# Two heads' chunk matrices side by side on one diagonal, inverted and folded together, in a one-core RWKV-7 + sparse-attention layer

## The chip, the cores and the metric

The kernel runs on one core of one Trainium2 chip. The metric is the device time of one execution in microseconds (us). The core has five engines that run side by side and wait for one another through semaphores: PE (TensorE, the matrix multiplier; its weight loads are listed apart as PEld), DVE (VectorE), ACT (ScalarE), POOL (GpSimd) and SP (SyncE, which here issues the transfers).

## What is computed

One layer of a decoder: 512 prompt tokens and 64 sample tokens (8 requests of 8), width 1024, with two token mixers on the same normalised input, a gated merge, an output projection and a SwiGLU network. The change lies in the first mixer, RWKV-7, whose state S (64x64 for each of 8 heads) goes from token to token:

```
def step(S, inp):
    r_t, w_t, k_t, v_t, a_t, b_t = inp
    sa = einsum('bhij,bhj->bhi', S, a_t)
    S = S * w_t[:, :, None, :] + sa[..., None] * b_t[:, :, None, :] + v_t[..., None] * k_t[:, :, None, :]
    return S, einsum('bhij,bhj->bhi', S, r_t)
```

The kernel takes 64 tokens at a time (a chunk). Within a chunk the term `sa` of a token depends on those of the tokens before it, which makes a triangular 64x64 system, identity minus N; its inverse is multiplied ("folded") into the read vectors, and then only 8 short steps for the prompt, and one for the samples, are left of the recurrence.

## The kernel before, in words

The 8 heads are worked on in 4 pairs i = 0..3, each with 9 chunks (8 of the prompt, the ninth of the samples), so 18 units of chunk and head. For each pair:

- `rw_operands` makes the scaled vectors, and by matmuls (L581, L592) the products of each chunk with itself. `pairs_out` masks them out of PSUM on DVE, in three instructions for four chunks of one head. The matrix N goes to partitions 64 to 127 of the tile `gb`, one 64x64 block for each of the 18 units.
- `rw_inverse` sends the four 16x16 diagonal blocks of each N through DRAM (`d1`) into 36 rows of the tile `im`, inverts them all with 30 DVE instructions (tiles `im`, `iw`, `invt`), and brings them back through DRAM (`d2`) into `gb`, `dt` (the tile `invt`), `b1` (named `b` in the rows) and `wt` (named `yb`). Its transfers are issued by SP in the order of its queue: 4 to `d1`, 1 from it, 2 to `d2`, 7 from it.
- `rw_merge_inverse` builds the 32x32 and then the 64x64 inverse from the blocks, on PE, in partitions 64 to 127, nine units (`u0` = 0, then 9) at a time: L661, evacuation L664, L668 and L671, evacuations L673 and L676, then L680, L683, L686, L688.
- `rw_transposed_reads` transposes the read vectors (L696) into `at`, a tile for each head, and `rw_fold_inverse` multiplies them by the inverse (L704), one product per unit, evacuates (L706), and clears the lower half of `gb` on POOL (L708).
- `rw_chain` runs the 8 steps (L803, L807, L812, L821), then the samples.

PE works on whatever the order gives it. Between the steps of the recurrence stand dense products of the input projection (L359, tile `pd`, here called fill): `spares` and `pull` hand out 26 tiles of it, by the tables `FILL` (how many tiles before chain i) and `PULL` (how many pieces after each half step). A list scheduler then orders all instructions on each engine; the functions `fold(i)` and parts of the chain have high priority in it. The fill counts 1968 dense matmuls up to its end, which lies within chain 3. After it come the attention heads (L1186 to L1227), the merge, the output projection and the feed-forward network, all with dense products on PE. Every 32-bit matmul of the small steps shows in the trace as two records, a transpose as one.

Of the kernel before, what the change touches and what calls it, by code (L numbers as in the profile page):

```python
# [13 lines left out]
F32R = mybir.dt.float32r  # L14
# [88 lines left out]
FILL = (12, 0, 6, 2)  # L103
PULL = (3, 5, 3, 2)
# [4 lines left out]
def tile_hybrid_step(ctx: ExitStack, tc: tile.TileContext, I: dict, O: dict):  # L109
# [372 lines left out]
    state, inv, bks = [], [], []  # L482

    def rw_tiles():

        state.extend(block(x, "state") for x in "XY")
        inv.extend(wide(x, x) for x in ("im", "iw"))
        bks.extend(wide(x, x) for x in ("bk0", "bk1"))

    def rw_state_tiles(i):  # L490
# [9 lines left out]
        S["agh"] = t_[:, 0:2 * w].rearrange("p (h c x) -> p c h x", h=2, c=9)  # L500
        S["lam"] = slots.t(32, "lam", "lam", 2).rearrange("p (h c) -> p h c", h=2)
        return S

    def pairs_out(pv_, mk, gb, ag):

        n = pv_.shape[1]
        for (rows, x) in ((slice(64, 128), 0), (slice(0, 64), 64)):
            tt(V, gb[rows], pv_[0:64, :, x:x + 64], bc(mk[0:64, None, x:x + 64], [64, n, 64]), ALU.mult)
        tt(V, ag[64:128], pv_[64:128], bc(mk[64:128, None, :], [64, n, 128]), ALU.mult)

    def rw_operands(S, i):
# [53 lines left out]
        for h in range(2):  # L565
# [27 lines left out]
        pairs_out(pt[:, 0:256].rearrange("p (h x) -> p h x", x=128), gmask[1], S["gb"][:, 8], S["agh"][:, 8])  # L593
# [11 lines left out]
    def rw_inverse(S):  # L605
# [32 lines left out]
        for k in range(2):
            o = 64 + k * 32
            G.tensor_copy(S["b1"][o:o + 16, :, 0:16], bc(ident[o:o + 16, None, o:o + 16], [16, NU, 16]))  # L640
            dma(S["dt"][o:o + 16], d2[1, k, :, 0].rearrange("u s t -> s u t"))
        for k in range(2):
            o = 64 + k * 32
            dma(S["b1"][o + 16:o + 32, :, 16:32], d2[0, k, :, 1].rearrange("u s t -> s u t"))
        dma(S["wt"][80:96, :, 16:32], d2[1, 0, :, 1].rearrange("u s t -> s u t"))
        for k in range(2):
            o = k * 32 + 16
            dma(gu[64 + o:80 + o, :, o:o + 16], d2[0, k, :, 1].rearrange("u s t -> s u t"))

    def rw_merge_inverse(S):  # L650

        gu, dt, b1, wt = S["gb"].rearrange("p c h x -> p (c h) x"), S["dt"], S["b1"], S["wt"]
        for k in range(2):
            o = k * 32
            G.tensor_copy(gu[64 + o:80 + o, :, o:o + 16], bc(ident[64 + o:80 + o, None, 64 + o:80 + o], [16, NU, 16]))
        for u0 in (0, 9):
            pz = PS(S["ct"])
            for u in range(9):
                for k in range(2):
                    o = k * 32  # L660
                    MM(pz[64 + o:96 + o, u * 16:u * 16 + 16], lhsT=gu[64 + o:80 + o, u0 + u, o:o + 32],  # L661
                       rhs=dt[64 + o:80 + o, u0 + u], start=True, stop=True)
            zt = slots.t(512, f"zt{S['i']}", f"zt{S['par']}")
            A.copy(zt[64:128, 0:144], pz[64:128, 0:144])  # L664
            pw = PS(S["ct"])
            for u in range(9):
                z0 = zt[64:96, u * 16:u * 16 + 16]
                MM(pw[64:96, 288 + u * 16:304 + u * 16], lhsT=b1[64:96, u0 + u], rhs=z0, start=True, stop=True)  # L668
                for k in range(2):
                    o = 64 + k * 32  # L670
                    MM(pw[o:o + 16, u * 32:u * 32 + 32], lhsT=zt[o:o + 32, u * 16:u * 16 + 16], rhs=b1[o:o + 32, u0 + u],  # L671
                       start=True, stop=True)
            V.tensor_copy(wt[64:96, u0:u0 + 9, 0:16], pw[64:96, 288:432].rearrange("p (u t) -> p u t", t=16))  # L673
            for k in range(2):
                o = k * 32
                A.copy(gu[64 + o:80 + o, u0:u0 + 9, o:o + 32], pw[64 + o:80 + o, 0:288].rearrange("p (u t) -> p u t", t=32))  # L676
        for u0 in (0, 9):
            pz = PS(S["ct"])
            for u in range(9):
# [1081 lines left out]
```

## Time and profile before

| | us |
|---|---|
| three runs | 1177.23, 1191.52 (median), 1199.91 |
| profiled execution | 1183.65 |
| its span, first to last instruction | 1181.8 |
| PE busy in it | 1128.9 (96%) |
| DVE busy | 729.4 (62%) |

A busy PE is not PE at its peak: matmuls overlap, and a stage of small ones is busy throughout. Start-to-start times in the timeline say more than durations. The column PEclk is the granted TensorE clock: 1.00 is 2.4 GHz, 0.50 is 1.2 GHz.

### The profile page before, as it was taken

Reading aid. Unit: us, or ns where it says so; the run is one execution under the profiler, and the core shown is the slowest. Engines: PE = TensorE matmul, PEld = TensorE weight load, DVE = VectorE, ACT = ScalarE, POOL = GpSimd, SP = SyncE. Lnnn points to the kernel's source line nnn. Section 1 sums busy time; section 2 is a strip of 40 time slices with the busy share of each in tenths; the row PEclk is TensorE's granted clock in tenths of the full one; section 3 lists DMA queues with packets and bytes.
Section 4 is the critical chain, followed back from the end, with each engine's and each line's share of the span. In section 5 each row is a group of like instructions: output and inputs, shape, how many; then the busy total and the mean of one; then the engine's idle time right before and its main releaser. Section 6 shows DMA issues by size and latency. Waiting matters only on the chain.

```text
span 1181.8 us, 23148 instructions
## 1 busy us (share of the span) xinstructions
PE 1128.9 (96%) x9117; PEld 1067.7 (90%) x9117; DVE 729.4 (62%) x1461; ACT 523.9 (44%) x1096; POOL 244.5 (21%) x313
## 2 busy tenths in 40 slices
PE   6999899999999999889999999999999999999995
PEld 5889899999888989777787999999999999999995
DVE  5484835359593754785677665697546754377554
ACT  4554533364533433675676433574223331234232
POOL 3333120024332221642254122100000100001000
PEclk9999999999987999899999999999999999999998
DMA  7223333222252353512331553314323242132222
GB/s 183 75 59 97 77 88 94 57 59 69 77 145 83 87 133 90 138 31 83 112 104 53 165 152 89 109 37 133 102 70 90 72 142 73 56 89 72 90 72 81
DMA packets 194792, 108.95 MB, mean 92 GB/s; under 512 B 49780, under 2 KB 187970, under 8 KB 194682
## 3 DMA queue, kind: packets, MB, share of 16 engines
q1 hardware_dynamic: 194682, 107.46, 32.7%
q8 instruction: 72, 1.18, 0.4%
q14 instruction: 38, 0.31, 0.1%
HBM read 91.40 MB, written 16.02 MB: 91 GB/s over the span
## 4 chain that ended last, share of the span: by engine, by line
PE 80%; DVE 8%; ACT 4%; DMA 4%; issue 2%; SPq 2%; POOL 0%; POOLq 0%; ACTq 0%; DVEq 0%
PE pd L359 46%; PE pu L359 10%; PE acc L1216 2%; PE ps L704 2%; PE ps L581 2%; SPq L152 1%; PE pT L1201 1%; PE ps L1037 1%; PE pS L1186 1%; DMA wraw<-in_w_in 1%; PE sm L396 1%; DVE invt L155 1%; PE pS L1188 1%; PE pq L733 1%; PE ps L696 1%
## 5 line engine op out<-in xcount | busy, mean ns | idle before, releaser
L359 PE MATMUL pd<-hh,whi 128*128 128x256 f32 (+1 forms) x656 | 203.7, 311 | 8.8 <-ACT pe L407 4.3
L359 PE MATMUL pd<-hh,wlo 128*128 128x256 f32 (+1 forms) x656 | 202.8, 309 | 2.7 <-DVE wlo L155 1.6
L359 PE MATMUL pd<-hl,whi 128*128 128x256 f32 (+1 forms) x656 | 201.5, 307 | 0.0
L359 PE MATMUL pd<-act,hi 128*128 128x288 f32 (+2 forms) x704 | 141.8, 296 | 0.0
L359 PEld LDWEIGHTS pd<-hh,whi 128*128 128x128 f32 x656 | 128.5, 196 | 11.9 <-ACT pe L407 6.3
L359 PEld LDWEIGHTS pd<-hh,wlo 128*128 128x128 f32 x656 | 128.5, 196 | 5.1 <-DVE wlo L155 2.0
L359 PEld LDWEIGHTS pd<-hl,whi 128*128 128x128 f32 x656 | 128.7, 196 | 1.4
L359 PEld LDWEIGHTS pd<-act,hi 128*128 128x128 f32 x704 | 112.6, 188 | 0.1
L155 DVE TENSOR_TENSOR wlo<-wraw,whi 128x1024 fp32r<-128x1024 f32 x60 | 81.0, 1351 | 43.8 <-ACT whi L337 40.0
L359 PE MATMUL pd<-act,lo 128*128 128x288 f32 (+2 forms) x352 | 103.8, 296 | 0.0
L359 PE MATMUL pd<-h2l,hi 128*128 128x288 f32 x352 | 103.6, 295 | 0.0
L359 PE MATMUL pd<-h2h,hi 128*128 128x288 f32 x352 | 103.1, 295 | 0.0
L359 PE MATMUL pd<-h2h,lo 128*128 128x288 f32 x352 | 103.1, 294 | 0.0
L337 ACT CAST hi<-wraw 128x1024 fp32r<-128x1024 f32 (+1 forms) x46 | 46.5, 1012 | 118.8 <-PE pd L359 62.5
L337 ACT CAST whi<-wraw 128x1024 fp32r<-128x1024 f32 x59 | 61.8, 1047 | 83.2 <-PE pd L359 52.7
L155 POOL TENSOR_TENSOR sg<-sg,ut 128x576 f32<-128x576 f32 x11 | 18.1, 1646 | 340.6 <-DVE ut L155 325.5
L155 DVE TENSOR_TENSOR x<-x,pd 128x288 f32<-128x288 f32 (+1 forms) x64 | 28.8, 451 | 65.4 <-PE pd L359 65.4
L155 DVE TENSOR_TENSOR lo<-wraw,hi 128x1024 fp32r<-128x1024 f32 (+1 forms) x46 | 57.0, 1240 | 19.0 <-ACT hi L337 18.8
L359 PEld LDWEIGHTS pd<-h2l,hi 128*128 128x128 f32 x352 | 66.1, 188 | 0.0
L359 PEld LDWEIGHTS pd<-act,lo 128*128 128x128 f32 x352 | 66.0, 188 | 0.0
L359 PEld LDWEIGHTS pd<-h2h,lo 128*128 128x128 f32 x352 | 66.0, 188 | 0.0
L359 PEld LDWEIGHTS pd<-h2h,hi 128*128 128x128 f32 x352 | 65.9, 188 | 0.0
(539 smaller groups left out, 2920.1 us busy)
## 6 DMA issues: line engine op xcount, KB each, us to landing
wraw<-in_w_in SPq DMA_DIRECT2D x35, 512.0 KB
wraw<-in_w_ffn_gate SPq DMA_DIRECT2D x22, 512.0 KB
ur<-in_w_ffn_up SPq DMA_DIRECT2D x44, 256.0 KB
wraw<-in_w_ffn_down SPq DMA_DIRECT2D x16, 512.0 KB
gt<-gsp SPq DMA_DIRECT2D x16, 288.0 KB
xt<-in_x_prompt SPq DMA_DIRECT2D x8, 512.0 KB
wraw<-in_w_out SPq DMA_DIRECT2D x8, 512.0 KB
wraw<-in_w_ffn_down SPq DMA_DIRECT2D x8, 384.0 KB
```

Of the source, the lines that this page charges most:

```text
L152: (eng or nc.sync).dma_start(out, in_)
L155: return e.tensor_tensor(out, a, b, op)
L337: e[0](hi[:, 0:n], raw[:, 0:n])
L359: i_ = MM(pt[:, 0:w_], lhsT=w, rhs=x[:, c], start=first and k == 0 and j == 0, stop=last and k == n - 1 and j == 2, **kw)
L396: MM(pt[:, 0:HALF], lhsT=l, rhs=r[:, half(a)], start=i == 0, stop=i == len(terms) - 1)
L581: MM(pt[:, c * 128:(c + 1) * 128], lhsT=bk[0:64, c0 + c], rhs=ag[:, c0 + c], start=True, stop=True)
L696: TR(pt[0:64, c * 128:c * 128 + 128], S["ag"][h][:, c0 + c, 0:64], ident)
L704: MM(pw[:, x * 64:x * 64 + 64], lhsT=S["at"][h][:, c], rhs=S["gb"][64:128, c, h], start=True, stop=True)
L733: MM(pq4[0:64, h, :, b], lhsT=s0s[h][0:64, b * 64:b * 64 + 64], rhs=rv[:, :, b], start=True, stop=True)
L1037: MM(po, lhsT=w[:, sl_], rhs=z[:, l, :, hf:hf + 162], start=hf == 0 and l == 0 and j == 0, stop=hf == 1 and l == 7 and j == 2)
L1186: MM(pS[:, 0:nk], lhsT=qs[:, qt * 128:qt * 128 + 128], rhs=kh[:, 0:nk], start=True, stop=False, skip_group_check=True)
L1216: MM(po[:, c0:hf * 256 + 256], lhsT=lv, rhs=ptx[m][:, kk * 256 + q0:kk * 256 + 256], start=name == "slc" and hf == 0 and kt == 0 and j == ...
```

## The change

The matrices N of both heads of a pair now go into one 128x128 tile per chunk, `nb`: head 0 in rows and columns 0 to 63, head 1 in 64 to 127, zeros elsewhere (set once). So there are 9 units instead of 18, and each of the 32-row quarters of PE holds a piece. The merge runs in one round over four quarters instead of two rounds over two. Both heads' transposed reads stand one above the other in one tile `at` of 128 partitions, and the fold is one product of 128x128 by 128x128 per chunk, for both heads. `gb` keeps zeros in its lower half for good, so the clearing after the fold goes. The transfers become twice as many where a head now has its own partitions (8, 1, 2 and 14 instead of 4, 1, 2 and 7), each of half the size. `pairs_out` is called once per head for the ninth chunk. The tiles `im` and `iw` shrink; the keys of the attention move into `bk0`, `bk1` and the values into `at0`, `at1`. `FILL` and `PULL` get other numbers, and the software DMA scratch is set to 2048.

```diff
-FILL = (12, 0, 6, 2)
-PULL = (3, 5, 3, 2)
+FILL = (10, 2, 6, 2)
+PULL = (4, 4, 3, 2)
...
-        inv.extend(wide(x, x) for x in ("im", "iw"))
+        inv.extend(slots.t(512, x) for x in ("im", "iw"))
...
+        nbs.extend(wide(x, x).rearrange("p (c x) -> p c x", x=128) for x in ("nb0", "nb1"))
+        ats.extend(wide(x, x).rearrange("p (c x) -> p c x", x=128) for x in ("at0", "at1"))
+        for t_ in nbs:
+            G.memset(t_, 0.0)
+        for t_ in state:
+            G.memset(t_[64:128, 4 * NTOK:8 * NTOK], 0.0)
...
-        for (rows, x) in ((slice(64, 128), 0), (slice(0, 64), 64)):
-            tt(V, gb[rows], pv_[0:64, :, x:x + 64], bc(mk[0:64, None, x:x + 64], [64, n, 64]), ALU.mult)
+        q = slice(h * 64, h * 64 + 64)
+        tt(V, nb[q, :, q], pv_[0:64, :, 0:64], bc(mk[0:64, None, 0:64], [64, n, 64]), ALU.mult)
+        tt(V, gb[0:64], pv_[0:64, :, 64:128], bc(mk[0:64, None, 64:128], [64, n, 64]), ALU.mult)
...
-        for k in range(2):
+        units = [(slice(h * 9, h * 9 + 9), k, h * 64 + k * 32) for h in range(2) for k in range(2)]
+        for u, k, o in units:
             for b in range(2):
-                o = k * 32 + b * 16
-                dma(d1[k, :, b].rearrange("u s t -> s u t"), gu[64 + o:80 + o, :, o:o + 16])
+                q = slice(o + b * 16, o + b * 16 + 16)
+                dma(d1[k, u, b].rearrange("u s t -> s u t"), nb[q, :, q])
...
+        for u, k, o in units:
+            G.tensor_copy(S["b1"][o:o + 16, :, 0:16], bc(ident[o:o + 16, None, o:o + 16], [16, 9, 16]))
+            dma(S["dt"][o:o + 16], d2[1, k, u, 0].rearrange("u s t -> s u t"))
+        for u, k, o in units:
+            dma(S["b1"][o + 16:o + 32, :, 16:32], d2[0, k, u, 1].rearrange("u s t -> s u t"))
+            if k == 0:
+                dma(S["wt"][o + 16:o + 32, :, 16:32], d2[1, 0, u, 1].rearrange("u s t -> s u t"))
+        for u, k, o in units:
+            q = slice(o + 16, o + 32)
+            dma(nb[q, :, q], d2[0, k, u, 1].rearrange("u s t -> s u t"))
...
+        quarters, halves = (0, 32, 64, 96), (0, 64)
...
+        for u in range(9):
+            for o in quarters:
+                MM(pz[o:o + 32, u * 16:u * 16 + 16], lhsT=nb[o:o + 16, u, o:o + 32], rhs=dt[o:o + 16, u], start=True, stop=True)
...
+            for o in quarters:
+                MM(pw[o:o + 16, u * 32:u * 32 + 32], lhsT=z[o:o + 32], rhs=b1[o:o + 32, u], start=True, stop=True)
+            for o in halves:
+                MM(pw[o:o + 32, 288 + u * 16:304 + u * 16], lhsT=b1[o:o + 32, u], rhs=z[o:o + 32], start=True, stop=True)
...
+            for o in halves:
+                MM(pz[o + 32:o + 64, u * 32:u * 32 + 32], lhsT=nb[o:o + 32, u, o + 32:o + 64], rhs=wt[o:o + 32, u],
...
+                MM(pw[o:o + 32, u * 32:u * 32 + 32], lhsT=zt[q, u * 32:u * 32 + 32], rhs=nb[q, u, q], start=True, stop=True)
...
-        for cs in ([(c, 0) for c in range(8)], [(c, 1) for c in range(8)], [(8, h) for h in range(2)]):
+        for c0 in (0, 4, 8):
+            m = min(4, 9 - c0)
             pw = PS(S["ct"])
-            for x, (c, h) in enumerate(cs):
-                MM(pw[:, x * 64:x * 64 + 64], lhsT=S["at"][h][:, c], rhs=S["gb"][64:128, c, h], start=True, stop=True)
...
-        G.memset(S["gb"][64:128], 0.0)
+            for c in range(m):
+                MM(pw[:, c * 128:c * 128 + 128], lhsT=S["at"][:, c0 + c], rhs=S["nb"][:, c0 + c], start=True, stop=True)
```

Below, pieces of the order of instructions are shown; the number after a tile's name only tells one buffer from another. First PE at the fold of pair 0, before: `im` and `iw` are the two heads' transposed reads, `state` holds the inverse, and `pd` is fill.

```order
958 L704 MATMUL ps_1585<-state_316,im_318 128x64 x3
959 L704 MATMUL ps_1595<-state_316,iw_319 128x64 x8
960 L600 MATMUL ps_1342<-ident_63,bk_85_320 128x64
961 L600 MATMUL ps_1342<-ident_63,bk_86_321 128x64
962 L696 MATMUL ps_1424<-ident_63,state_317 64x128 x4
963 L359 MATMUL pd_2070<-hh_98,wlo_2039 128x320
964 L359 MATMUL pd_2070<-hh_100,whi_2038 128x320
965 L359 MATMUL pd_2070<-hl_101,whi_2038 128x320
966 L704 MATMUL ps_1605<-state_316,im_318 128x64
```

The same place on PE now (L715 is the fold):

```order
934 L359 MATMUL pd_2095<-hl_97,whi_2063 128x320
935 L359 MATMUL pd_2095<-hh_96,wlo_2064 128x320
936 L715 MATMUL ps_1620<-nb_87_322,at_89_324 128x128 x4
937 L715 MATMUL ps_1626<-nb_87_322,at_89_324 128x128 x4
938 L612 MATMUL ps_1369<-ident_63,bk_85_320 128x64
939 L612 MATMUL ps_1369<-ident_63,bk_86_321 128x64
940 L706 MATMUL ps_1467<-ident_63,state_317 64x128
941 L706 MATMUL ps_1470<-ident_63,state_317 64x128
```

The products of 64 columns become half as many of 128 columns, from one pair of tiles. The next piece is SP's queue where pair 0's inverse comes back from DRAM, before (`state` is `gb`):

```order
136 L152 DMA d2p_158_897<-iw_319 36x512
137 L152 DMA d2p_158_897<-im_318 36x512
138 L152 DMA nsp<-nsp_1879 128x320
139 L152 DMA b_160_940<-d2p_158_897 16x18x16
140 L152 DMA invt_906<-d2p_158_897 16x18x16 x2
141 L152 DMA b_160_940<-d2p_158_897 16x18x16
142 L152 DMA yb_941<-d2p_158_897 16x18x16
143 L152 DMA state_316<-d2p_158_897 16x18x16 x2
```

And now:

```order
136 L152 DMA d2p_162_908<-iw_319 36x512
137 L152 DMA d2p_162_908<-im_318 36x512
138 L152 DMA nsp<-nsp_1994 128x320
139 L152 DMA b_164_955<-d2p_162_908 16x9x16
140 L152 DMA invt_921<-d2p_162_908 16x9x16 x4
141 L152 DMA yb_956<-d2p_162_908 16x9x16
142 L152 DMA b_164_955<-d2p_162_908 16x9x16 x2
143 L152 DMA yb_956<-d2p_162_908 16x9x16
144 L152 DMA b_164_955<-d2p_162_908 16x9x16
145 L152 DMA nb_87_322<-d2p_162_908 16x9x16 x4
```

Seven transfers become fourteen in the same place of the queue. Over the whole program the order has 311 places, instead of 285, at which PE passes between fill and another matmul before the fill ends, and four steps of chain 3, instead of three, begin after the end of the fill.

## Rows read from the trace of the kernel before

**Rows 1.** The page's first two parts: busy time of each engine, then the granted clock of PE in 40 slices of the span, in tenths.

```profile
PE 1128.9 (96%) x9117; PEld 1067.7 (90%) x9117; DVE 729.4 (62%) x1461; ACT 523.9 (44%) x1096; POOL 244.5 (21%) x313
...
PEclk9999999999987999899999999999999999999998
```

**Rows 2.** The chain of work that ended last, by engine, shares of the span.

```profile
PE 80%; DVE 8%; ACT 4%; DMA 4%; issue 2%; SPq 2%; POOL 0%; POOLq 0%; ACTq 0%; DVEq 0%
```

**Rows 3.** Windows of 100 us and more: from:to, length, busy us (instructions) of PE, PEld, DVE, ACT, POOL, then the granted clock, the DMA share and GB/s.

```profile
100.00:200.00 100.00, 95.68 (x938) 90.12 (x937) 55.13 (x133) 42.35 (x84) 22.12 (x38) 0.97 0.35 86
200.00:300.00 100.00, 100.00 (x934) 94.90 (x933) 59.92 (x123) 46.57 (x99) 24.40 (x25) 0.98 0.23 63
300.00:400.00 100.00, 97.50 (x902) 90.00 (x901) 60.66 (x133) 43.32 (x87) 32.32 (x40) 0.90 0.39 104
400.00:500.00 100.00, 94.50 (x879) 86.30 (x877) 61.99 (x153) 43.63 (x114) 30.40 (x38) 0.91 0.45 118
```

**Rows 4.** The timeline of PE at the fold (L704) of pair 0, and at four transposes with a full 128x128 operand (L848): start us, us from the first start to the last end, and the count of records.

```profile
178.56 1.61 PE L704 MATMUL ps<-state,iw 64*128 64x64 f32 x13
...
354.88 0.66 PE L848 MATMUL ps<-ident,yb 128*128 128x128 f32 x4
```

**Rows 5.** Groups by line and shape on PE: busy us, mean ns of one record, idle before.

```profile
L704 PE MATMUL ps<-state,bk 64*128 64x64 f32 x72 | 10.1, 284 | 0.0
...
L686 PE MATMUL ps<-state,zt 32*32 32x32 f32 x144 | 6.2, 192 | 0.0
L704 PE MATMUL ps<-state,iw 64*128 64x64 f32 x36 | 6.2, 330 | 0.0
...
L704 PE MATMUL ps<-state,im 64*128 64x64 f32 x36 | 5.5, 288 | 0.0
```

**Rows 6.** The timeline of PE in the merge: 16-column products that alternate between two 32-row quarters (L661), 32-column products in one quarter (L686).

```profile
159.68 0.71 PE L661 MATMUL ps<-invt,state 16*32 16x16 f32 x35
...
174.10 0.75 PE L686 MATMUL ps<-state,zt 32*32 32x32 f32 x18
```

**Rows 7.** The timeline of PE where it passes from fill to eight small products (64 rows) and back.

```profile
151.92 0.31 PE L359 MATMUL pd<-hh,whi 128*128 128x320 f32 x1
152.07 0.30 PE L359 MATMUL pd<-hl,whi 128*128 128x320 f32 x1
152.30 1.16 PE L581 MATMUL ps<-state,bk 64*128 64x128 f32 x8
153.39 0.42 PE L359 MATMUL pd<-hh,wlo 128*128 128x320 f32 x1
153.64 0.31 PE L359 MATMUL pd<-hh,whi 128*128 128x320 f32 x1
```

**Rows 8.** SP's queue at pair 0: the issue of the four transfers to `d1`, then of the seven back from `d2`.

```profile
113.00 2.06 SPq L152 DMA_DIRECT2D d1p<-state  x4
...
150.62 0.32 SPq L152 DMA_DIRECT2D b<-d2p  x1
151.04 0.90 SPq L152 DMA_DIRECT2D invt<-d2p  x2
151.99 0.44 SPq L152 DMA_DIRECT2D b<-d2p  x1
152.53 0.40 SPq L152 DMA_DIRECT2D yb<-d2p  x1
152.97 0.95 SPq L152 DMA_DIRECT2D state<-d2p  x2
```

**Rows 9.** DVE's three instructions of `pairs_out` for the ninth chunk.

```profile
112.57 1.04 DVE L155 TENSOR_TENSOR state<-ps,mat 64x128 f32<-64x128 f32 x3
```

**Rows 10.** POOL's clearing after the fold (ns: least, median, most; then first and last start).

```profile
L708 POOL MEMSET state<- x4: 1052/1054/1063, 182.3 to 442.8; 64x1152 f32 x4
```

**Rows 11.** Windows of 5 us where PE stood idle or the granted clock fell, and one (175 to 180) where it did not (columns as in rows 3).

```profile
130.00:135.00 5.00, 1.67 (x10) 1.46 (x10) 4.77 (x20) 4.50 (x9) 0.52 (x3) 0.95 0.15 49
...
160.00:165.00 5.00, 5.00 (x55) 4.43 (x49) 2.95 (x5) 2.80 (x6) 0.00 (x0) 0.68 0.51 141
...
175.00:180.00 5.00, 5.00 (x43) 4.74 (x44) 1.50 (x8) 1.87 (x5) 0.42 (x1) 1.00 0.17 43
...
335.00:340.00 5.00, 2.50 (x19) 2.19 (x18) 4.96 (x10) 0.95 (x3) 1.11 (x2) 0.93 0.49 126
...
370.00:375.00 5.00, 5.00 (x49) 4.64 (x46) 1.65 (x4) 1.56 (x3) 0.00 (x0) 0.85 0.62 166
375.00:380.00 5.00, 5.00 (x26) 4.43 (x26) 1.53 (x3) 1.43 (x3) 2.60 (x2) 0.50 0.00 1
380.00:385.00 5.00, 5.00 (x33) 4.71 (x32) 1.06 (x4) 0.72 (x2) 1.34 (x5) 0.63 0.08 26
425.00:430.00 5.00, 5.00 (x50) 4.47 (x50) 4.21 (x9) 1.04 (x3) 0.43 (x2) 0.69 0.76 200
440.00:445.00 5.00, 5.00 (x29) 4.23 (x29) 1.23 (x1) 2.89 (x7) 1.05 (x1) 0.67 0.00 0
445.00:450.00 5.00, 5.00 (x30) 5.00 (x31) 0.28 (x1) 0.66 (x2) 0.00 (x0) 0.64 0.59 162
485.00:490.00 5.00, 2.01 (x13) 1.59 (x13) 3.70 (x13) 2.61 (x10) 4.62 (x9) 0.95 0.38 87
```

**Rows 12.** The steps of chain 3 (L803, tile `qy3c`): duration of one record in ns, first and last start in us.

```profile
L803 PE MATMUL qy3c<-state x32: 217/275/422, 445.6 to 495.8; 128*128 128x64 f32 x32
```

More of the change, by code (lines that the diff above doesn't have):

```diff
@@ L592, in rw_operands @@
             MM(pt[:, h * 128:(h + 1) * 128], lhsT=bk2[h][0:64, 8], rhs=S["ag"][h][0:64, 8], start=True, stop=True)
-        pairs_out(pt[:, 0:256].rearrange("p (h x) -> p h x", x=128), gmask[1], S["gb"][:, 8], S["agh"][:, 8])
+        p3 = pt[:, 0:256].rearrange("p (h x) -> p h x", x=128)
+        for h in range(2):
+            pairs_out(p3[:, h:h + 1], gmask[1], h, S["nb"][:, 8:9], S["gb"][:, 8:9, h], S["ag"][h][:, 8:9])
         for h in range(2):
@@ L608, in rw_inverse @@
         d2 = scratch.tile([2, 2, NU, 2, 16, 16], F32, name=nm(f"d2p{S['i']}"), tag="d2", bufs=2)
-        gu = S["gb"].rearrange("p c h x -> p (c h) x")
+        nb = S["nb"]
         mt, wt = inv
-        S["at"] = [t_[64:128].rearrange("p (c x) -> p c x", x=128) for t_ in (bks if S["par"] else inv)]
         n = 2 * NU
@@ L636, in rw_inverse @@
-        for t_ in (S["b1"][64:128], S["wt"][64:96]):
+        S["wt"] = S["yb"][:, 0:288].rearrange("p (u t) -> p u t", t=32)
+        for t_ in (S["b1"], S["wt"]):
             tc.add_manual_dep(G.memset(t_, 0.0).ins, S["scaled"].ins.name, ORDER, reason="behind the scalings")
[L638 to L648, printed above, removed]
-    def rw_merge_inverse(S):
[L652 to L679, printed above, removed]
-                MM(pz[96:128, u * 32:u * 32 + 32], lhsT=gu[64:96, u0 + u, 32:64], rhs=wt[64:96, u0 + u],
-                   start=True, stop=True)
-            zt = slots.t(512, f"zt{S['i']}", f"zt{S['par']}")
-            A.copy(zt[96:128, 0:288], pz[96:128, 0:288])
-            pw = PS(S["ct"])
-            for u in range(9):
-                MM(pw[64:96, u * 32:u * 32 + 32], lhsT=zt[96:128, u * 32:u * 32 + 32], rhs=gu[96:128, u0 + u, 32:64],
-                   start=True, stop=True)
-            A.copy(gu[64:96, u0:u0 + 9, 32:64], pw[64:96, 0:288].rearrange("p (u t) -> p u t", t=32))
@@ L690, in rw_transposed_reads @@
     def rw_transposed_reads(S):
-        for h in range(2):
-            for c0 in (0, 4, 8):
-                m = min(4, 9 - c0)
+        for c0 in (0, 4, 8):
+            m = min(4, 9 - c0)
+            for h in range(2):
                 pt = PS(S["ct"])
@@ L1097, in ns_operands @@
             vr = projected(2 * bi + 1, C(name="vraw"))
-            vt = wide(f"bk{bi}", "vtok")
+            vt = wide(f"at{bi}", "vtok")
             N.setdefault("vt", []).append(vt)
@@ L1742 @@
     from concourse.bass_utils import run_bass_kernel_spmd
[L1744 removed]
+    nc = bacc.Bacc("TRN2", target_bir_lowering=False, num_devices=1, dynamic_dma_scratch_size=2048)
     arrays, ins, outs = {}, {}, {}
```

49 lines of the change are left out of this document (37 added, 12 removed).

## The prediction

> **What bounds the kernel now.** I read the page first. PE is busy for 96% of the span and no other engine for more than 62% [rows 1], and the chain that ended last is PE for 80% of it [rows 2]. So this is a kernel of PE work, and the question is whether the stage of the change is that too. The windows say that it is: from 100 to 500 us, where all four pairs are worked on, PE is busy 388 of 400 us, with DVE at 55 to 62 and ACT at 42 to 47 in each 100 [rows 3]. The reader is to see there that the recurrence, a chain full of waits, is already covered: between its steps PE does fill. A wait that becomes shorter in this stage is worth little; PE time that goes is worth all of itself, as long as fill is left. What spoils the picture is the granted clock: 0.90 and 0.91 in the second half of the stage [rows 3], with single windows at 0.50, which is 1.2 GHz, although PE was busy in them [rows 11].
>
> **The change part by part.**
>
> *The fold.* It has 72 + 36 + 36 = 144 records [rows 5], 36 products for each pair. Thirteen of them take 1.61 us; less the length of one (0.28 us, by the mean of 284 ns) that is 1.33 / 12 = 0.111 us from start to start [rows 4, 5]. Now there are 9 products for each pair, 72 records, with a full 128x128 operand and 128 columns. The nearest row is a transpose with the same operand and columns: (0.66 - 0.28) / 3 = 0.127 us [rows 4]. So 144 x 0.111 - 72 x 0.127 = 16.0 - 9.1 = 6.8 us less. A product may cost more than a transpose. If a record with twice the columns took twice as long, nothing would be gained; if it took the old 0.111, 8.0 us would be. I take the transpose's value, since its operand and columns are the same.
>
> *The second half of the merge.* L686 works in one quarter of PE, with 32 columns: (0.75 - 0.19) / 17 = 0.033 us from start to start [rows 5, 6]. L680 has as many products, by the code, so 288 records in all. Now they alternate between two quarters. Where two quarters already alternate (L661, 16 columns) it is (0.71 - 0.19) / 34 = 0.015 us [rows 6]. I take 0.020, near that row because of the alternation and above it because of the columns: 288 x 0.013 = 3.7 us less. Ends: 0, if a quarter's neighbour doesn't help, and 288 x 0.018 = 5.2.
>
> *The first half of the merge.* The number of products stays, and two quarters at 0.015 us become four. I take no gain: for so few columns the row is about what starting a record costs. If four quarters ran twice as fast as two, the 288 records of L661's kind would give 288 x 0.008 = 2.3 us more, and a loss is not excluded by more than the same.
>
> The Trainium skill ("TensorE: Matmul & The Clock Gate", section "Wait — 56ns, not 53.3ns?") speaks against the last two terms: start-to-start of matmuls is said never to drop below about 25 ns, however few columns. The trace does not agree, with its 15 ns for L661. By the rule the second half of the merge would come to 288 x 8 ns = 2.3 us less, and the sum below would be 1.4 us smaller.
>
> *Passing between fill and small products.* From one fill matmul to the next of 320 columns it is 0.15 us; from fill to the first small product 0.23, and from the first fill matmul after them to the second 0.25 [rows 7]. So each passage costs about 0.09 us. The order now has 311 passages instead of 285 before the end of the fill: 26 x 0.09 = 2.3 us more. The ends are 0 and 26 x 0.25 = 6.5. This is where the Trainium skill ("TensorEngine Tiling (Array Packing)", "Key Properties") agrees with the trace: a change of tiling mode, not of tile alone, is said to drain the engine. It gives no time.
>
> *SP and DMA.* Eleven more transfers for each pair, at 2.06 / 4 = 0.5 us each on the way to DRAM and 3.0 / 7 = 0.43 back [rows 8]: 4 x 0.5 + 7 x 0.43 = 5.0 us later for each pair's inverse. Queued behind them on SP are the rows of projected columns, stored to DRAM, and the next weights of the fill. Those are needed by PE only when the fill before them is through. I cost this at nothing: what hides it is fill on PE, which stands in the order between each pair's inverse and its merge. Without the cover it is 20 us for four pairs.
>
> *DVE and POOL.* The ninth chunk costs six DVE instructions instead of three. Three take 1.04 us [rows 9]; split by head, six take no less than that and no more than twice as much, so 1 us for a pair at most. POOL loses four clearings of 1.05 us [rows 10] between a fold and the chain that needs it, and gets as much clearing once at the start. Both are under PE's fill: nothing, and if the cover is gone 4 us either way. The moved keys and values, the smaller tiles, the scratch size and the tables change when things run, not how much of them: nothing, beyond the passages counted.
>
> *Sum.* -6.8 - 3.7 + 2.3 = -8 us. Against the profiled execution's own 1183.65 us that is 1176. That execution lay below the median of the three runs, 1191.52; the mean of all four times is 1188, and I forecast from there: 1180 us. By the ends of the terms the sum goes from about +9 (the fold gains nothing, neither half of the merge does, each passage costs 0.25 us and the first half loses 2.3) to -16.
>
> **The rivals.**
>
> *The gain is given back at the end of the recurrence (1188 us).* The order begins four steps of chain 3 after the end of the fill instead of three. A step takes (495.8 - 445.6) / 7 = 7.2 us [rows 12]. If one step lies open, 7 of the 8 us are gone. For it: PE is idle 3 of 5 us at 485 [rows 11], where the fill has just ended. Against it: attention heads stand there in the order too, and need no chain 3.
>
> *Slower: the inverse comes later than the fill can cover (1202 us).* Each pair's inverse is 5.0 us later by SP and up to 1.0 by DVE, 5.4 with half of the latter; four pairs in a row, 22 us, against a gain of 8: 1188 - 8 + 22 = 1202. It decides as soon as more than 2 us of the 5.4 stay open for each pair. For it: PE idles 3.3 us at 130 and 2.5 at 335, while DVE is full (4.77 and 4.96 of 5) with the next pair's operands and inverse [rows 11], so there the fill waits for DVE's half of the weights and the cover is thin. Against it: those are two windows in 400 us.
>
> *The clock stays up (1168 us).* The windows with a fold or merge in them and a clock below 1 lose, as length times what is missing of the clock: 1.6 us at 160, 0.75 + 2.5 + 1.85 at 370 to 385, 1.55 at 425, 1.65 + 1.8 at 440 to 450, in all 11.7 us [rows 11]. In 375 to 380 PE was busy throughout, at 1.2 GHz, after a stretch of folds with 64 rows and 64 columns. If shorter stretches of fuller products keep the clock up, 12 us more are gained: 1188 - 8 - 12 = 1168. Against it: from 175 to 180, with half of pair 0's fold, the same products of the same size, the clock is 1.00 [rows 4, 11], so the fold alone doesn't do it.
>
> **How the numbers follow.** The forecast has 0.5, the gain given back 0.2, the slower case 0.14, the clock 0.16. The range has to take in 1168 and 1202 with some scatter of the three runs, which lie 23 us apart: 1160 to 1204, and about a tenth of each outer case is left out. Two per cent of the median, about what a measurement of this kernel can tell from no change, is 24 us: 1168 and 1215. Half of the clock's case and a little scatter of the forecast make "faster" 0.13; a quarter of the slower case and scatter make "slower" 0.06; the rest is 0.81.
>
> **What would show it.** The fold's group should have 72 records about 0.127 us apart. The second half of the merge should run at about 0.02 us from start to start, and the first half at 0.015 as before. The fill should end some 8 us earlier, and all that follows should move by that. The windows of 100 to 500 us should show PE no less busy. I am wrong about the fold if its records are 0.2 us apart; about the cover if PE is idle for more than the 12 us that it is now between 100 and 500; and about the clock if its mean there is off by more than 0.02 from now.

## The result: 42 us less, where 8 were forecast

The changed kernel takes 1146.05 us (median of four, 1145.26 to 1152.49), the kernel before 1187.72 (median of four): ratio 0.969, 95% interval 0.9605 to 0.9774. The prediction, 1180 within 1160 to 1204, was wrong. The kernel before was also run beside the experiments, in four groups; over these 48 executions its median is 1189.4 (1186 to 1192 by group), and against that the gain is 43 us. Executions in the slower state are left out here and below.

The page of the changed kernel has as much of PE as before, as a share, and a granted clock without the two gaps that [rows 1] shows:

```profile
PE 1098.8 (96%) x9045; PEld 1038.5 (91%) x9045; DVE 732.0 (64%) x1473; ACT 520.8 (46%) x1092; POOL 246.2 (22%) x329
...
PEclk9999999999999999999999999999999999999998
...
PE 83%; DVE 8%; ACT 4%; issue 2%; SPq 1%; DMA 1%; POOL 1%; POOLq 0%; DVEq 0%; ACTq 0%
```

The last line is the chain that ended last, by engine: PE is 83% of it, 80% in [rows 2]. Next the windows of the changed kernel, columns as in [rows 3], and below the first four some shorter ones, at its idle time and at its folds:

```profile
100.00:200.00 100.00, 95.40 (x988) 90.19 (x989) 57.05 (x143) 42.41 (x85) 21.38 (x45) 0.98 0.36 87
200.00:300.00 100.00, 100.00 (x925) 93.64 (x924) 67.07 (x145) 50.39 (x107) 31.00 (x39) 1.00 0.27 71
300.00:400.00 100.00, 97.34 (x1119) 90.26 (x1120) 83.14 (x171) 47.74 (x99) 31.79 (x36) 0.98 0.49 134
400.00:500.00 100.00, 95.24 (x745) 82.87 (x745) 63.35 (x169) 57.53 (x160) 35.26 (x54) 0.91 0.36 92
...
125.00:130.00 5.00, 2.24 (x20) 2.04 (x18) 4.70 (x15) 4.79 (x11) 1.83 (x3) 1.00 0.00 0
130.00:135.00 5.00, 4.12 (x19) 4.12 (x20) 4.90 (x11) 1.87 (x4) 2.99 (x2) 0.72 0.23 75
170.00:175.00 5.00, 5.00 (x41) 4.81 (x40) 0.00 (x0) 2.52 (x6) 2.27 (x8) 1.00 0.19 26
215.00:220.00 5.00, 5.00 (x41) 5.00 (x40) 1.07 (x4) 1.64 (x4) 0.00 (x0) 1.00 0.02 2
415.00:420.00 5.00, 5.00 (x31) 4.91 (x31) 0.08 (x1) 0.93 (x2) 1.03 (x1) 0.66 0.30 85
```

PE is busy for 388.0 of the 400 us, as in [rows 3]; the clock between 300 and 400 us is 0.98 instead of 0.90. Between 400 and 500 us it is 0.91 in both, but there the changed kernel has passed the end of its fill (444 us), and the work is another. The stretches at 1.2 GHz behind folds and merges [rows 11] are gone but for one (415 us, where a fold and sample products stand side by side). The idle time that [rows 11] have at 130 us is still there, now from 127 to 131 us, with DVE nearly full; the clock falls behind it (0.72).

The timeline of PE in the merge and the fold of pair 0 (L670 was L661, L687 was L680, L715 was L704; columns as in [rows 4, 6]):

```profile
153.81 0.74 PE L670 MATMUL ps<-invt,nb 16*32 16x16 f32 x66
...
162.34 0.75 PE L687 MATMUL ps<-yb,nb 32*32 32x32 f32 x34
...
170.90 1.95 PE L715 MATMUL ps<-nb,at 128*128 128x128 f32 x16
```

From start to start the records are (0.74 - 0.18) / 65 = 0.0086 us where [rows 6] have 0.015, (0.75 - 0.19) / 33 = 0.017 where [rows 6] have 0.033, and (1.95 - 0.28) / 15 = 0.111 for the fold, the same as for the half-size product of [rows 4]. SP's queue (start, us of issue) and the steps of chain 3:

```profile
110.14 4.84 SPq L152 DMA_DIRECT2D d1p<-nb  x8
...
148.19 0.32 SPq L152 DMA_DIRECT2D b<-d2p  x1
...
152.83 3.10 SPq L152 DMA_DIRECT2D nb<-d2p  x4
```

```profile
L812 PE MATMUL qy3c<-state x32: 218/275/422, 414.0 to 461.0; 128*128 128x64 f32 x32
```

Eight transfers take 4.84 us to issue where four took 2.06, and the fourteen back 7.74 us (to 155.93) where seven took 3.3 [rows 8]. Chain 3 starts its last step at 461.0 us instead of 495.8 [rows 12].

**Two parts of a time.** A trace gives for every execution the span and the mean granted clock. Since the clock in the traces is either 2.4 or 1.2 GHz, the time at 1.2 GHz is 2 x (1 - mean clock) x span. If PE works all through it, half of it is lost; the span less that half is called *rest* here. In the 48 executions of the kernel before, the time scatters by 4.4 us (standard deviation), the time at 1.2 GHz by 11.3 and the rest by 2.5, and the first two go together (correlation 0.91): most of what differs from run to run is clock. But a straight line through them rises by 0.35 us, not 0.5, for each us at 1.2 GHz. So part of the loss is made up elsewhere; what is put to the clock below, at a half, is an upper value, and what is put to the rest a lower one.

| medians, us | time | at 1.2 GHz | rest |
|---|---|---|---|
| before | 1189.4 | 78 | 1147.1 |
| changed | 1146.0 | 34 | 1127.8 |

Of the 43 us, about 19 are rest and 22 are clock by the half (44 x 0.35 = 15 by the line). The profiles can be followed to the end of the fill, which comes at 444.4 instead of 478.2 us: added up from the starts of all PE records, the work at full clock went from 431.3 to 418.4 us, idle time from 17.5 to 14.3, time at 1.2 GHz from 44 to 10. The 12.9 of work, the 3.2 of idle time and half of the 34 at 1.2 GHz make up 33 of the 33.8 us.

### The profile page after: what moved, and what is told of

Its sections match the earlier page's. It is cut to its first block, busy times and chain, and to the rows that moved or that the text cites. A ratio compares the mean times of both kernels' runs of the same rounds, so it can differ in the third digit from the quotient of the medians.

```text
span 1143.2 us, 23074 instructions
## 1 busy us (share of the span) xinstructions
PE 1098.8 (96%) x9045; PEld 1038.5 (91%) x9045; DVE 732.0 (64%) x1473; ACT 520.8 (46%) x1092; POOL 246.2 (22%) x329
## 4 chain that ended last, share of the span: by engine, by line
PE 83%; DVE 8%; ACT 4%; issue 2%; SPq 1%; DMA 1%; POOL 1%; POOLq 0%; DVEq 0%; ACTq 0%
PE pd L359 50%; PE pu L359 10%; PE acc L1225 2%; PE ps L590 1%; SPq L152 1%; PE ps L1046 1%; PE pT L1210 1%; PE pS L1195 1%; PE sm L396 1%; DVE state L578 1%; PE ps L706 1%; PE ps L715 1%; PE pS L1197 1%; PE pTs L1319 1%; PE ps L772 1%
## 5 line engine op out<-in xcount | busy, mean ns | idle before, releaser
L359 PE MATMUL pd<-hh,whi 128*128 128x256 f32 (+1 forms) x656 | 200.9, 306 | 8.7 <-ACT pe L407 4.7
L359 PE MATMUL pd<-hh,wlo 128*128 128x256 f32 (+1 forms) x656 | 198.9, 303 | 1.7 <-DVE wlo L155 1.6
L359 PE MATMUL pd<-hl,whi 128*128 128x256 f32 (+1 forms) x656 | 199.2, 304 | 0.0
L359 PEld LDWEIGHTS pd<-hh,whi 128*128 128x128 f32 x656 | 125.5, 191 | 11.7 <-ACT pe L407 5.9
L359 PEld LDWEIGHTS pd<-hh,wlo 128*128 128x128 f32 x656 | 125.2, 191 | 3.8 <-DVE wlo L155 2.0
L359 PEld LDWEIGHTS pd<-hl,whi 128*128 128x128 f32 x656 | 125.4, 191 | 1.4
L155 DVE TENSOR_TENSOR wlo<-wraw,whi 128x1024 fp32r<-128x1024 f32 x60 | 78.6, 1310 | 39.6 <-ACT whi L337 39.2
```

Of the source, the lines that this page charges most:

```text
L155: return e.tensor_tensor(out, a, b, op)
L359: i_ = MM(pt[:, 0:w_], lhsT=w, rhs=x[:, c], start=first and k == 0 and j == 0, stop=last and k == n - 1 and j == 2, **kw)
```

## The experiments

In the expectations, S says that the shapes of merge and fold save both PE work and clock, T that the tables keep the clock up, M and F that merge or fold alone does, N that the merge's rounds were hidden, O that the places of the falls are chance of the order; a fall is a place where the granted clock goes from 2.4 to 1.2 GHz. The expectations of e5 to e16 say what their letters mean (F is another one in e7 and e8).

### Is it the tables or the structure?

e1 is the changed kernel with the old tables, e2 the kernel before with the new ones.

```diff
# e1, on the changed kernel (e2: the reverse on the kernel before)
-FILL = (10, 2, 6, 2)
-PULL = (4, 4, 3, 2)
+FILL = (12, 0, 6, 2)
+PULL = (3, 5, 3, 2)
```

> The changed kernel with the fill tables of before, FILL (12, 0, 6, 2) and PULL (3, 5, 3, 2). Theory S (the gain is PE work of the merge and the fold, and the clock that stays up because of their shape): the tables have no part, 1140 to 1155 us, and no fall of the clock within 5 us behind a merge or a fold of pairs 0 to 3. Rival T (the other spread of the fill is what keeps the clock up): most of the 17 us of clock are lost again, 1160 us or more, with falls behind merges and folds. Rival O (chance of the order that the scheduler makes): anything, with falls at other places than in either kernel.

> The kernel before with the fill tables of the changed one. Theory S: 1180 to 1195 us, 400 of 1000 of the falls' time still behind merges and folds, at least four falls there between 100 us and the end of the fill. Rival T: 1165 us or less, and at most two falls there. Rival O: between the two, with falls at places that have nothing to do with the merge and the fold.

Measured: e1 1160.5 us (ratio to before 0.977, 0.9728 to 0.9812), e2 1167.7 (0.9843, 0.9805 to 0.9881). Both count: each lies outside what S forecast, and each keeps a part of the gain. The work of PE up to the end of the fill goes with the structure alone: 416.3 us in e1, 430.5 in e2. Three more pairs of tables were run on both structures: e7 to e10 with one old table and one new, e11 and e12 with FILL (9, 3, 6, 2) and the new PULL.

> The changed kernel with FILL back at (12, 0, 6, 2) and PULL left at the new (4, 4, 3, 2). Both back cost 14.3 us (1160.5). Theory F (FILL is the one that counts: two fill steps of pair 0 moved behind the place where the second pair's operands are built): 1157 to 1161, idle of TensorE up to the end of the fill near 23 us. Theory P (PULL counts): 1146 to 1149, idle near 14 us. If both count: about 1153.

> The changed kernel with PULL back at (3, 5, 3, 2) and FILL left at the new (10, 2, 6, 2). Theory F: 1146 to 1149, idle near 14 us. Theory P: 1157 to 1161, idle near 23 us, with waits of TensorE for VectorE at the chain steps and samples as in e1. If both count: about 1153. If the two alone come out beyond both ends (together better or worse than either), the tables work only by where the falls land.

> The kernel before with FILL (12, 0, 6, 2) and PULL (4, 4, 3, 2), to stand beside e7, the changed kernel with the same tables. For every run of a kernel, its time at 1.2 GHz is 2 x (1 - mean granted clock) x span, and the rest is the span less half of that. So far, as medians: tables old, structure old 78 us at 1.2 GHz and rest 1146.5, structure new (e1) 46 and 1135.0; tables new, structure old (e2) 47 and 1142.6, new 34 and 1127.8; e7 72 and 1136.8. Both theories: rest 11 to 15 us above e7's, about 1150. Theory K (the new shapes of merge and fold keep the clock up, whatever the order): 1.2 GHz for 12 to 32 us more than in e7, so about 92 us, a time of 1198. Theory O (the clock's loss comes with the order that each kernel happens to have, the shapes have no part): anywhere between 34 and 78 us, as likely below e7's 72 as above; at 55 us a time of 1179.

> The kernel before with FILL (10, 2, 6, 2) and PULL (3, 5, 3, 2), to stand beside e8 (same tables, structure new: 38 us at 1.2 GHz, rest 1132.4, time 1153.0). Both theories: rest about 1145. Theory K: 50 to 70 us at 1.2 GHz, a time of 1172 to 1182. Theory O: 34 to 78 us, with no lean to the upper side. One pair decides little; with e1, after and e7 beside their partners it is four pairs, and theory K wants the old structure above in all of them, theory O in about half.

> The kernel before with tables that neither kernel has: FILL (9, 3, 6, 2), PULL (4, 4, 3, 2). Beside e12 a fifth pair. Rest 1141 to 1146. Theory K: 12 to 32 us more at 1.2 GHz than e12, and a time 21 to 30 us above e12's. Theory O: the difference of the time is 13 us for the rest, and up to 18 us more or less for the clock.

> The changed kernel with FILL (9, 3, 6, 2), PULL (4, 4, 3, 2): one more fill step moved from ahead of chain 0 to behind it. If moving steps there goes on to fill TensorE's idle time (12 to 10 took 5 to 9 us of the rest): rest 1124 to 1127, and at 34 us of 1.2 GHz a time of 1143 to 1146. If the new tables are simply a good one of many orders: rest 1128 to 1133, 40 to 60 us at 1.2 GHz, a time of 1150 to 1165.

| FILL, PULL | old structure: time, 1.2 GHz, rest | new structure | difference |
|---|---|---|---|
| old, old | before 1189.4, 78, 1147.1 | e1 1160.5, 46, 1135.0 | -28.9 |
| old, new | e9 1197.6, 81, 1155.1 | e7 1174.9, 72, 1136.8 | -22.7 |
| new, old | e10 1178.0, 54, 1149.9 | e8 1153.0, 38, 1132.4 | -25.0 |
| new, new | e2 1167.7, 47, 1142.6 | changed 1146.0, 34, 1127.8 | -21.7 |
| third | e11 1187.1, 73, 1148.2 | e12 1163.3, 75, 1125.2 | -23.8 |

Read by rows, the structure is worth 22 to 29 us whatever the tables are, 24 in the mean: 12 to 23 of rest, and in four of five pairs 10 to 32 us less at 1.2 GHz (e11 and e12: none). Theory K wanted all five, so it is borne out in four by the sign; e12 has the low rest that was hoped for (1125.2) and twice the time at 1.2 GHz. Read by columns, the new tables are worth 22 us on the old structure and 14 on the new, the best of the five on both; theories F and P of e7 and e8 both fall, since FILL alone put back costs 29 us, PULL alone 7, and both together 14. Part of it is idle time (up to the end of the fill 22.9 us in e1, 14.3 in the changed kernel), and PE's waits show where. First the changed kernel, then e1, 100 to 480 us (engine, line, releaser: us in total, times, longest):

```profile
PE pd L359 <- ACT nsp L896: 3.6, 1, 3.6
PE pS L1195 <- ACT P L1204: 2.0, 2, 1.9
PE qy2c L821 <- DVE state L816: 1.3, 1, 1.3
...
PE qy1c L763 <- DVE state L761: 0.7, 1, 0.7
```

```profile
PE qy2c L821 <- DVE state L816: 4.5, 2, 4.0
PE pd L359 <- ACT nsp L896: 3.6, 1, 3.6
PE qy1c L763 <- DVE state L761: 3.0, 1, 3.0
```

With the old tables PE waits 5.5 us more for DVE, at the steps and samples of chains 1 and 2. The clock's part of the tables is another matter. In e7 PE falls to 1.2 GHz at 473.6 us, in the last chain's steps behind the end of the fill (464.4), where it had been idle for 3.0 us of the 5 before (2.2 for DVE, 0.8 for ACT). It stays there until 511, through 20 us in which it is busy throughout (e7, then the changed kernel, whose fill ended 20 us earlier):

```profile
470.00:475.00 5.00, 2.32 (x11) 1.65 (x12) 3.12 (x12) 1.99 (x7) 4.36 (x11) 0.86 0.39 103
480.00:500.00 20.00, 20.00 (x104) 16.85 (x104) 8.52 (x24) 7.77 (x26) 6.57 (x9) 0.50 0.14 37
500.00:520.00 20.00, 18.47 (x98) 15.33 (x98) 15.36 (x37) 12.94 (x35) 7.88 (x11) 0.72 0.14 30
```

```profile
480.00:500.00 20.00, 17.43 (x101) 13.45 (x101) 17.00 (x42) 14.56 (x38) 8.08 (x12) 0.83 0.29 69
500.00:520.00 20.00, 19.29 (x133) 15.90 (x132) 11.03 (x37) 10.58 (x34) 4.77 (x9) 1.00 0.33 95
```

If the end of the fill were the weak place in general, fill moved to the last chain should help. e15 (PULL (4, 4, 2, 2)) and e16 (FILL (10, 2, 5, 3)) tried it on the changed kernel.

> The changed kernel with PULL (4, 4, 2, 2): one piece of fill less after each half step of chain 2, all of it later. If the small products of the last chain and its samples are what loses the clock and waits at the end of the fill, they get cover: less than 34 us at 1.2 GHz, rest 1124 to 1128, 1138 to 1145 us. If the order's chance decides: rest 1128 to 1133 and 40 to 60 us, 1150 to 1162.

> The changed kernel with FILL (10, 2, 5, 3): a sixteenth of the fill's pulls moved from ahead of chain 2 to ahead of chain 3. The same two theories: cover for the last chain 1138 to 1145 us; chance of the order 1150 to 1162; and with less fill ahead of chain 2 a wait of TensorE for the third inverse there, of 2 to 6 us, if that is what the two now behind chain 1 cover.

Measured: e15 1166.8 us (0.9794, 0.972 to 0.9869; 72 at 1.2 GHz, rest 1130.3), e16 1163.2 (0.9772, 0.9703 to 0.9842; 58, 1131.8). Neither helps: both lie above the 1150 to 1162 us that were expected if the order's chance decides. PE also waits for the inverse there, 1.9 us in e15 and 1.4 in e16 for transfers back from `d2`. No version that was tried beats the changed kernel. Its tables are the best of seven on this structure (the other six: 1153 to 1175 us), and no single wait was found that makes them so. That the order's chance is a large part of their worth is the reading that fits, not a mechanism shown. It has a consequence for all that follows: an edit of the changed kernel also leaves the best of seven orders, and can lose by that alone.

### The fold alone

e3 cuts the changed kernel's fold into 18 products per pair of 64 rows and 64 columns, as before, with one evacuation more. e13 does the same to e1, e14 to e8, so there are three pairs that differ in nothing else, two of them on tables that are not the best.

```diff
-        for c0 in (0, 4, 8):
+        for cs in ([(c, 0) for c in range(8)], [(c, 1) for c in range(8)], [(8, 0)], [(8, 1)]):
...
-                MM(pw[:, c * 128:c * 128 + 128], lhsT=S["at"][:, c0 + c], rhs=S["nb"][:, c0 + c], start=True, stop=True)
+                q = slice(h * 64, h * 64 + 64)
+                MM(pw[:, x * 64:x * 64 + 64], lhsT=S["at"][q, c], rhs=S["nb"][q, c, q], start=True, stop=True)
```

> The changed kernel with its fold alone undone: one product of 64 rows and 64 columns per chunk and head, 144 records again instead of 72, with one small evacuation more per pair. Theory S: the work of PE comes back, 8 to 9 us by the records' spacing, and the falls of the clock behind the folds of pairs 2 and 3 come back (10.2 and 6.8 us long before, so up to 8.5 us): 1154 to 1163 us. Rival M (the clock is kept up by the merge's shape, the fold has no part in it): the work alone, 1153 to 1156, and no fall behind a fold. Rival O: falls at other places.

> e1 (changed kernel with the old tables: 1160.5 us, 46 us at 1.2 GHz, rest 1135.0) with the fold in 18 products of 64 rows x 64 columns as in e3. Both theories: rest +8 to +9 (in e3 +9), 1144. Theory K (half-size folds bring the clock down, whatever the order): 10 to 28 us more at 1.2 GHz, falls behind at least one of the four folds, 1160.5 + 9 + 5 to 14 = 1175 to 1184. Theory O (falls only change place): 46 us within 12, 1163 to 1176.

> e8 (changed kernel with PULL old: 1153.0 us, 38 us at 1.2 GHz, rest 1132.4) with the fold in 18 products of 64 rows x 64 columns. Both: rest about 1141. Theory K: 48 to 66 us at 1.2 GHz, falls behind at least one fold, 1167 to 1176. Theory O: 26 to 50 us, 1156 to 1168.

| tables | full-size fold | half-size fold | difference: time, 1.2 GHz, rest |
|---|---|---|---|
| new, new | changed 1146.0 | e3 1169.4 (ratio 0.9859, 0.9803 to 0.9916) | +23.4, +28, +8.9 |
| old, old | e1 1160.5 | e13 1183.9 (0.9996, 0.9952 to 1.004) | +23.4, +25, +11.7 |
| new, old | e8 1153.0 | e14 1186.2 (0.9964, 0.9927 to 1.0) | +33.2, +51, +7.0 |

With the old tables this one edit gives back 23.4 of the 28.9 us that the structure won; with the two other pairs of tables it gives back more than all (23.4 of 21.7, 33.2 of 25.0). The rests came near what was expected. The time at 1.2 GHz came higher in e3 and e14, whose times lie above all that was forecast for them (1153 to 1163 and 1156 to 1176 us); e13 lies within theory K's range. Where the time goes is seen at the folds of pairs 0, 1 and 3. Windows of e1 (folds from 173.0, 217.2 and 418.0 us), then of e13 (172.9, 214.9 and 427.7), columns as in [rows 3]:

```profile
175.00:180.00 5.00, 5.00 (x42) 4.93 (x43) 2.02 (x6) 2.73 (x7) 0.30 (x1) 1.00 0.17 53
...
215.00:220.00 5.00, 5.00 (x43) 5.00 (x42) 0.49 (x2) 1.54 (x3) 0.00 (x0) 1.00 0.53 134
220.00:225.00 5.00, 5.00 (x42) 5.00 (x41) 2.56 (x6) 2.11 (x5) 1.27 (x1) 1.00 0.00 0
...
420.00:425.00 5.00, 5.00 (x42) 5.00 (x42) 1.71 (x6) 2.02 (x6) 0.00 (x0) 1.00 0.62 182
```

```profile
175.00:180.00 5.00, 5.00 (x29) 4.48 (x29) 1.62 (x8) 2.31 (x7) 0.31 (x1) 0.67 0.07 20
215.00:220.00 5.00, 5.00 (x37) 4.70 (x37) 1.11 (x4) 0.84 (x2) 0.00 (x0) 0.77 0.11 24
220.00:225.00 5.00, 5.00 (x20) 4.55 (x21) 0.00 (x0) 0.80 (x2) 0.00 (x0) 0.55 0.00 0
...
435.00:440.00 5.00, 5.00 (x19) 4.33 (x18) 0.28 (x1) 0.21 (x1) 0.00 (x0) 0.55 0.00 0
```

PE is busy for all 5 us in both; at and behind the half-size products the clock is at 1.2 GHz for part of each window, at the full-size ones in none of these. The timeline of e3 at pair 0 shows the price in the fill that follows:

```profile
171.30 0.31 PE L359 MATMUL pd<-hl,whi 128*128 128x320 f32 x1
171.45 0.31 PE L359 MATMUL pd<-hh,wlo 128*128 128x320 f32 x1
171.69 3.05 PE L715 MATMUL ps<-nb,at 64*128 64x64 f32 x29
...
175.53 0.47 PE L359 MATMUL pd<-hl,whi 128*128 128x320 f32 x1
175.80 0.47 PE L359 MATMUL pd<-hh,wlo 128*128 128x320 f32 x1
```

The same fill matmul starts 0.15 us after its neighbour ahead of the fold and 0.27 behind it. Over all profiles, one execution of each kernel, 19 of the 32 folds made of half-size products have a fall of the clock before their last product ends, with PE busy throughout or nearly (at most 0.9 us idle in the 5 us ahead). Of the 40 with more rows or columns one has a fall right behind it (two of these 40 ran at 1.2 GHz already).

Is it the rows or the columns? e6 cuts the changed kernel's fold by columns alone, 128 rows x 64; e5 widens the fold of the kernel before to 128 columns of which 64 are thrown away, with 64 rows as they were.

```diff
# e6, on the changed kernel
+                for x in (0, 64):
+                    MM(pw[:, c * 128 + x:c * 128 + x + 64], lhsT=S["at"][:, c0 + c], rhs=S["nb"][:, c0 + c, x:x + 64], ...)
# e5, on the kernel before
-                MM(pw[:, x * 64:x * 64 + 64], lhsT=S["at"][h][:, c], rhs=S["gb"][64:128, c, h], start=True, stop=True)
+                MM(pw[:, x * 128:x * 128 + 128], lhsT=S["at"][g][:, c], rhs=S["btgb"][64:128, c, g], start=True, stop=True)
```

> The changed kernel, with its fold product cut by columns alone: two products of 128 rows x 64 columns per chunk in place of one of 128 x 128, 144 records a layer of two heads each where there were 72, same evacuations, same tables. With e3 (64 rows x 64 columns, 39.5 us of 1.2 GHz up to the end of the fill against 9.8, and falls behind three of four folds, 1169.4 us) this tells rows from columns. PE work: +72 records of about 0.103 us = +7.4 us. Theory W (width in columns keeps the clock up): falls behind the folds as in e3, 10 to 24 us of 1.2 GHz more, 1146 + 7 + 5 to 12 = 1158 to 1165 us. Theory R (rows keep it up): no fall behind a fold, 1146 + 7 = 1153 us.

> The kernel before, with one thing changed: each record of the fold streams 128 columns instead of 64 (the right operand is the whole 128-column block of the chunk, of which the second half is kept and the first thrown away), so a pair has five evacuations in place of three. Rows stay 64, the tables stay old, the result is the reference's. In the kernel before, two of its four folds are followed by a stretch at 1.2 GHz (373.5 us, 10.2 us long, and 441.7 us, 6.8 us long). Theory W (the products' width in columns keeps the clock up): no fall behind any fold; 17.0 us of 1.2 GHz gone, worth up to 8.5 us; the 144 records cost up to 16 ns more each, +2.3 us, and two more evacuations per pair about +0.5: 1180 us, -6 against the kernel before. Theory R (rows, or rows and columns together, decide): falls behind two of the four folds as before, 1186 + 2.8 = 1189 us. Theory O (where the clock falls is chance of the order): some falls at other places, 1189 within 6.

Measured: e6 1164.0 us (0.9784, 0.973 to 0.9837; 45 at 1.2 GHz, rest 1138.1). No fall stands at any of its folds, as theory R has it, but 11 us more at 1.2 GHz came at other places, and the rest is 10 higher, of which 7.0 are PE work as expected; so the time is not R's 1153 but lies where theory W wanted it. e5 1190.2 (1.002, 0.9982 to 1.0058; 74, 1152.1): no fall at a fold either, as theory W has it, and still no gain; the rest is 5 us higher and the time at 1.2 GHz hardly lower (74 instead of 78). Its profile shows where some of it came back, though it is of the fastest of its executions (1177.8 us, 45 at 1.2 GHz):

```profile
370.00:375.00 5.00, 5.00 (x42) 4.31 (x41) 1.53 (x3) 1.59 (x4) 2.42 (x2) 1.00 0.11 34
375.00:380.00 5.00, 5.00 (x39) 4.55 (x38) 1.28 (x4) 0.97 (x2) 3.58 (x10) 1.00 0.23 41
400.00:405.00 5.00, 2.51 (x20) 2.29 (x19) 3.84 (x6) 4.44 (x8) 0.00 (x0) 0.87 0.29 47
405.00:410.00 5.00, 5.00 (x52) 4.63 (x52) 1.63 (x6) 1.18 (x5) 0.00 (x0) 0.50 0.67 180
410.00:415.00 5.00, 5.00 (x66) 4.46 (x66) 4.53 (x10) 0.39 (x2) 2.83 (x3) 0.50 0.56 141
```

At 375 us, where the clock of the kernel before is 0.50 [rows 11], it is 1.00. But PE waits 2.5 us at 400, where the kernel before has no wait, falls to 1.2 GHz there and stays at it past 415. So with either dimension in full no fall came at the folds themselves, in the seven of these two profiles that did not run at 1.2 GHz already; the time that this should save came back at other places. Only with the full-size fold was it kept.

### The merge alone

e4 is the changed kernel with its merge in two rounds, one head after the other.

```diff
-        pz = PS(ct)
-        for u in range(9):
+        for h in range(2):
+            quarters, halves, hh = (h * 64, h * 64 + 32), (h * 64,), slice(h * 64, h * 64 + 64)
+            pz = PS(ct)
...
```

> The changed kernel with its merge in two rounds again, one head after the other, each round with its own PSUM tile and evacuations, the fold as changed. Theory S: the merge's products run as before, 24.8 us instead of 16.8 for all pairs by their spacing, and falls behind the merge come back (three of 3.4 us before, 5 us lost): 1154 to 1160 us. Rival F (the clock is a matter of the fold alone): 1153 to 1155 with no fall behind a merge. Rival N (the rounds are hidden by fill and the spacing is a matter of which quarters alternate, which stays within a head): 1146 to 1150.

Measured: 1157.6 us (0.9776, 0.9723 to 0.9829), +11.6 to the changed kernel: PE work +7.8 in the profile, rest +4.9, 12 us more at 1.2 GHz. The time is theory S's, but the falls behind the merge that S wanted are not separable: those at 325 and 404 us stand behind the merge's first products and behind idle time both (2.3 and 2.2 us of the 5 ahead, for DVE in the chain). Undoing the fold (23.4) and the merge (11.6) costs more together than the structure is worth with these tables (21.7), so each also loses some of what the order had.

That the new merge's shape keeps the clock up does not hold. Eleven profiles have it, and in all of them PE runs the same records in the same order from the program's start to the fill behind the merge of pair 0 (157.7 us in the changed kernel). Four of them (e1, e7, e13, e15) fall to 1.2 GHz there, at about 156 us and with PE busy throughout, the other seven do not. The changed kernel, then e1:

```profile
155.00:160.00 5.00, 5.00 (x142) 4.84 (x143) 3.46 (x7) 2.45 (x5) 1.89 (x1) 1.00 0.65 140
```

```profile
155.00:160.00 5.00, 5.00 (x69) 4.69 (x59) 2.24 (x4) 2.24 (x4) 1.89 (x1) 0.66 0.56 119
```

So neither the shape nor the order decides a single fall, and it takes many places, or the clock of many executions, to judge a shape.

## Why the prediction was wrong, step by step

- *What bounds it: right.* PE work that goes was worth all of itself, and 388 of 400 us are busy as before. The rival of a later inverse did not come: SP's two stretches are 7.2 us longer instead of 5.0, and none of PE's waits between 100 and 480 us is for these transfers (with the tables of e15 and e16 some are). Nor did the rival of a gain given back at the end of the recurrence: in the 60 us behind the end of the fill PE is idle for 4.8 us instead of 6.4.
- *The fold's work: sized low.* 0.111 us a record instead of 0.127. The transposes that gave the 0.127 were no guide; the old product was. In all four shapes that were run, 64 or 128 rows by 64 or 128 columns, the median from one fold record to the next is 0.112 us, so half the records is half the time; all four load 128 columns of weights (188 to 192 ns), which no run changed. Added up from the starts of all records, at full clock, 16.8 us became 8.0: -8.8, not -6.8.
- *The second half of the merge: nearly.* 0.017 us against 0.020 within a run of records. Over all of them it is 0.034 and now 0.025, since the order cuts the runs with fill: 9.9 us became 7.3, -2.6 instead of -3.7.
- *The first half: failed.* It was costed at nothing because 15 ns was taken for what starting a record costs. Four quarters take 8.6 ns: L661 with its successor went from 6.5 to 4.5 us, L668 and L671 from 8.4 to 5.0, together -5.4. The end of 2.3 that the text allowed counted L661's 288 records alone; the 432 of L668 and L671 stood in no term. The floor of 25 ns that the Trainium skill states ("TensorE: Matmul & The Clock Gate", section "Wait — 56ns, not 53.3ns?") does not hold for these products: the trace has 8.6 ns.
- *Passages: right.* The fill's own records take 2.9 us more, 2.3 forecast.
- *The clock: failed.* It was a rival at 0.16 and nothing in the sum. What spoke against it was one window, half a fold at 1.00. One case in which the clock stayed up does not show that it always will: 19 of 32 such folds had a fall. The mean clock between 100 and 500 us went from 0.94 to 0.97, more than the 0.02 that the text set as its own limit. The fold alone, by three pairs, is worth 23 to 33 us, about 9 of them rest and 12 to 25 clock by the half. So the rival's mechanism, fuller products that keep the clock up, is borne out for the fold, and not for the merge.
- *The tables: failed.* They "change when things run, not how much": costed at nothing. On the new structure they are worth 14 us, on the old one 22.

So the structure brought 24 us (22 to 29) where 8 were forecast, and the tables 14 to 22 where none were. What is open: what makes this one pair of tables good, how much of the clock's gain belongs to the merge, and why the same records are followed by a fall in one execution and not in another.

## What to carry to other kernels

Split every execution into rest and clock before explaining a difference: here the rest was steady within 2.5 us, and most of the scatter went with the clock. Test the half by a line through many executions of one kernel; here it was 0.35. Where PE is always busy, look for stretches at 1.2 GHz at runs of products that fill a part of the array, and judge them over all such places, not by one. A change that comes with other numbers for the order is two changes: run each with the other's numbers, since order alone was worth up to 30 us here.

## What the runs showed of the hardware beyond expectation

- Records of products of 16 rows and 16 columns that take turns on four 32-row quarters start 8.6 ns apart, on two quarters 15 ns.
- A fold record of 128 rows x 128 columns and one of 64 x 64 cost nearly the same from start to start: 0.111 us in the changed kernel, (3.05 - 0.28) / 28 = 0.099 in e3 at pair 0, and by the median of all folds 0.112 in both.
- The granted clock can lie at 1.2 GHz for a whole 20 us in which PE is busy for 20.00 (e7, 480 us), in sample and attention products behind the end of the fill.
- The same PE records in the same order are followed by a fall of the clock in 4 of 11 profiles and by none in 7 (at 156 us, behind the merge of pair 0).
